# Head norms of a gated DeltaNet branch: sums over channels as two products with ones, and their way from tokens to a row

## The chip, the cores and the metric

One Trainium2 chip, one core. The time is that of one execution in device microseconds, as the median of repeated runs. The kernel takes the whole layer in one launch.

## The reference, cut to what matters

A hybrid encoder layer with three parallel branches (gated DeltaNet, latent attention, cross-attention to a memory) of width 1024 with 8 heads of 128 channels in the branch that matters here, for two inputs of 256 tokens each. The kernel treats both inputs as one stretch of 512 tokens. The change is in the last step of the DeltaNet branch: its output o is normed per head and token over the 128 channels, and then gated.

```python
def _rmsnorm(x, gain):
    xf = x.astype(jnp.float32)
    y = xf * lax.rsqrt(jnp.mean(xf * xf, axis=-1, keepdims=True) + EPS)
    return (y * gain.astype(jnp.float32)).astype(x.dtype)
...
o_gdn = _rmsnorm(o_fwd + o_bwd, gdn_norm_gain).reshape(b, s, W_GDN).astype(x.dtype) * jax.nn.silu(z_gdn)
...
merged = (gates[:, :, 0] * (o_gdn @ w_br_gdn) + gates[:, :, 1] * (o_mla @ w_br_mla) + gates[:, :, 2] * (o_mem @ w_br_mem))
return x + merged @ w_out
```

## The kernel before, in words

Nearly all values lie with channels on the 128 partitions and the 512 tokens along the row. Big products are made in three passes of a reduced float type: each operand is split into a high and a low part (`split`, L216: a ScalarE copy at L219 rounds to the high part, a VectorE subtraction at L221 or L223 gives the rest; weights in the same way at L207 and L211), and high*high, high*low and low*high are summed in PSUM. Such a product is one generator, `gemm` (L243 issues the matmuls, tiles `gm_...`); 24 matmuls of 128x512 make one output block of 128 channels.

The program has a front, a middle and a back (`run`). In the middle, `weave` merges seven chains (preparation, loads, the inner part of each head, two lanes that solve the recurrences, `heads_out`, `heads_norm`) with the stream of big products. Every chain yields two numbers: the TensorE time that it has just issued and how long to stay away. As long as no chain is due, `weave` issues the next matmul of the big products and moves its clock on by 0.234. TensorE's order is what `weave` writes down. The other engines' orders come from a scheduler that goes by priorities, which each chain sets as an offset (`heads_out` 2000, `heads_norm` 1500), and by `issue_after`, which keeps an instruction behind the last split of a weight (`wround`: its ScalarE half, `wsplit`: its VectorE half). Each engine then works strictly in its own order.

For each head hh, `gdn_out` (from L1100) does this:

- o, eight matmuls at L1117 in one PSUM bank; og = o * gain * z at L1124 (VectorE), o squared into sq at L1126 (ScalarE), a second square added at L1127 and L1129, so that the term with EPS is right; then the chain stays away for 11 (13 for head 7).
- so, the sums over channels, at L1133: for each block of 128 tokens a float32 matmul with sq as the stationary operand and a column of ones as the moving one. The trace counts eight weight loads and eight matmuls for the four. The result is 128x4, a token on each partition.
- rr at L1135 (VectorE, 128x4), to the power -0.5 at L1136 (GpSimd), turned in blocks of 32x32 at L285 (VectorE), so that four rows of each block of 32 partitions hold the tokens, and four DMAs from SyncE's queue at L287 put them in order into one row of the DRAM buffer `d_n`.

`gdn_norm` (from L1141) reads that row back to all 128 partitions (`rob`, a DMA that ScalarE issues at L292, behind `wround`), multiplies og by it at L1149 (behind `wsplit`), and splits the result into `xg` (L219, L223). `xg` is read in the back by the products `gm_bg`. The back starts when the last products `gm_bm` of the middle have been issued.

Small tiles share buffers by tags: `ta`, `tb` and `ct` have two buffers each of 128x512. `tb` holds sq and rob. `ct` holds the gates `gt_...` and `zt_...` on their way to DRAM, and `cz`, the raw tiles of the convolution (L733, L743). A new tile with a tag waits until everything that reads the tile before the last has ended.

Of the kernel before, what the change touches and what calls it, by code (L numbers as in the profile page):

```python
# [7 lines left out]
F32 = mybir.dt.float32  # L8
F32R = mybir.dt.float32r
AF = mybir.ActivationFunctionType  # L10
ALU = mybir.AluOpType
AX = mybir.AxisListType

P = 128
# [3 lines left out]
EPS = 1e-6  # L18
# [137 lines left out]
class Layer:  # L156
# [34 lines left out]
    def c(self, n):  # L191
        lo, hi = _OFF[n]
        return self.cst[:, lo:hi]
# [82 lines left out]
    def bcast(self, r, ps):  # L276

        for tb in range(4):
            self.nc.tensor.matmul(ps[:, tb * P:(tb + 1) * P], r[:, tb:tb + 1].to_broadcast([P, P]),
                                  self.c("id"), start=True, stop=True)  # L280

    def store_cols(self, r, i):

        nc = self.nc
        nc.vector.transpose(out=self.rt, in_=r)  # L285
        for b in range(4):
            nc.sync.dma_start(self.d_n[i].rearrange("(j b i) -> b j i", j=4, b=4)[b], self.rt[32 * b:32 * b + 4])  # L287

    def load_row(self, dst, i):

# [809 lines left out]
    def gdn_out(self, hh):  # L1100

        nc, pg, c = self.nc, self.pg, self.c
        par, kq = hh % 2, self.kq[hh]
        (na, es, vt), ub = self.hd[hh], self.ub[hh]

        op = self.ps_ms(par, f"o{hh}")
        o3 = op.rearrange("p (s t) -> p s t", s=2)
        for s in range(2):
            n = 0
            for d in range(2):  # L1110
                for cp in range(2):
                    if cp == 0:
                        out, rhs = o3[:, s], es[d][:, s, 0:256]
                    else:
                        lo = 128 * (1 - d)
                        out, rhs = o3[:, s, lo:lo + 128], es[d][:, s, 256:384]
                    nc.tensor.matmul(out, ub[:, d, s, cp], rhs, start=n == 0, stop=n == 3)  # L1117
                    n += 1
            yield 1.3, 0.0

        og = self.ta(f"og{hh}")
        nc.sync.dma_start(og, self.d_z[:, hh])
        self.out = hh + 1
        nc.vector.scalar_tensor_tensor(og, op, self.gg, og, ALU.mult, ALU.mult)  # L1124
        sq = self.tb(f"sq{hh}")
        nc.scalar.activation(sq, op, AF.Square)  # L1126
        nc.scalar.activation(kq[:, :, 1], kq[:, :, 1], AF.Square, scale=0.064)  # L1127
        s3 = sq.rearrange("p (s t) -> p s t", s=2)
        nc.vector.tensor_tensor(s3, s3, kq[:, :, 1], op=ALU.add)  # L1129
        yield 0.0, 13 if hh == 7 else 11  # L1130
        ssp = self.ps_ms(par, f"so{hh}")
        for tb in range(4):
            nc.tensor.matmul(ssp[:, tb:tb + 1], sq[:, tb * P:(tb + 1) * P], c("one"), start=True, stop=True)  # L1133
        rr = self.rr[:, 0:4]
        nc.vector.tensor_scalar(rr, ssp[:, 0:4], 1.0 / 128, 128 * EPS * EPS, ALU.mult, ALU.add)  # L1135
        nc.gpsimd.tensor_tensor(rr, rr, c("hf")[:, 0:4], op=ALU.pow)  # L1136
        self.store_cols(self.rr, hh)
        self.og[hh] = og, self.now + 10.0
        yield 0.9, 0.0

    def gdn_norm(self, hh):  # L1141

        nc = self.nc
        og = self.og[hh][0]
        rb = self.tb(f"rob{hh}")
        self.load_row(rb, hh)
        yield 0.0, 6.0
        with self.tc.issue_after(self.wsplit):
            nc.vector.tensor_tensor(og, og, rb, op=ALU.mult)  # L1149
        hl = self.pk.tile([P, 2, 512], F32R, tag="kq", bufs=8, name=f"xg{hh}")  # L1150
        self.split(og, hl[:, 0], hl[:, 1], 0.5)
        self.xg[hh] = hl[:, 0], hl[:, 1]
# [283 lines left out]
    def middle(self):  # L1436

        self.prepare(99)
        nc = self.nc
        fills = self.fills  # L1440

        self.ym = []
        for j in range(2):
            y = self.pg.tile([P, 2, 4, P], F32, tag=f"y{j}", bufs=1, name=f"y{j}")
            m = self.pg.tile([P, 2, P], F32, tag=f"m{j}", bufs=1, name=f"m{j}")
            nc.gpsimd.memset(y, 0.0)
            nc.gpsimd.memset(m, 0.0)
            self.ym.append((y, m))
        self.loads, self.loaded, self.started = {}, {}, set()
        self.og = {}  # L1450
        self.rr, self.rt = (self.p0.tile([P, 32], F32, name=n) for n in ("rr", "rt"))
        nc.gpsimd.memset(self.rr, 0.0)
        self.hd, self.ub, self.out, self.idle = {}, {}, 0, 0.0
        self.now, self.ready, self.pr = 0.0, {}, [None, None]
        with self.tc.manual_schedule(engines={mybir.EngineType.PE}):
            self.weave((self.preps(), 100), (self.heads_load(), 300), (self.heads_in(), 300), (self.lane(0), 2000), (self.lane(1), 2000),
                       (self.heads_out(), 2000), (self.heads_norm(), 1500))
# [153 lines left out]
```

## Time and profile before

| | before |
|---|---|
| median of 3 runs | 866.36 us (865.55 to 867.13) |
| profiled execution | 867.27 us, span 865.5 us, granted TensorE clock 0.995 |
| TensorE busy (PE) | 851.6 us of the span |
| VectorE busy (DVE) | 574.6 us |
| ScalarE busy (ACT) | 455.9 us |
| GpSimd busy (POOL) | 143.2 us |
| SyncE | issues DMAs only |

How to read it: PE is TensorE's matmul, PEld its weight loads, which overlap matmuls, DVE VectorE, ACT ScalarE, POOL GpSimd, SP SyncE; a letter q behind an engine's name is its queue of DMA issues. A row of the timeline gives the start, the duration of the whole group, the engine, the line, the operation with its output and inputs, its shape and how many instructions there are, and in brackets the idle time before it with what ended it. Matmuls are pipelined: a start is when a matmul begins, and the next one starts well before its end, so distances between starts tell what a matmul costs TensorE. A row of a group gives the line, engine, operation, shapes and count, then busy time in us, the mean of one in ns, and the idle time just before with its releaser.

### The profile page before, as it was taken

How to read it: one execution, taken by the hardware profiler on the slowest of the kernel's cores; microseconds unless marked ns; L12 is line 12 of the kernel's file. 1: busy time of each engine (PE TensorE's matmuls, PEld its weight loads, DVE VectorE, ACT ScalarE, POOL GpSimd, SP SyncE). 2: the span in 40 equal slices, each digit the busy share in tenths (PEclk: the TensorE clock that was granted, in tenths of full speed). 3: DMA queues.
4: the chain of work that ended last, by engine and by line, in shares of the span. 5: the costliest groups of instructions: out<-in, count | busy, mean ns of one | idle time of the engine just before them, and what ended most of it. 6: DMA issues, size and time to landing. Idle time of an engine off the chain costs nothing.

```text
span 865.5 us, 13255 instructions
## 1 busy us (share of the span) xinstructions
PE 851.6 (98%) x4854; PEld 703.0 (81%) x4854; DVE 574.6 (66%) x1013; ACT 455.9 (53%) x899; POOL 143.2 (17%) x135
## 2 busy tenths in 40 slices
PE   8999998999999999999999999999999999999997
PEld 6878887888888888878788888888888888888886
DVE  7776348876889865567689996765456543356543
ACT  7654454555655465545775647766563633223232
POOL 0200111000100100163011262303120002332121
PEclk9999999999999999999999999999999999999998
DMA  9322221452225423554232445544445436474432
GB/s 332 130 90 75 86 78 42 137 148 94 82 81 152 146 77 112 172 161 155 99 111 92 146 144 168 183 135 146 144 139 167 148 118 229 139 239 154 121 98 97
DMA packets 50864, 116.09 MB, mean 134 GB/s; under 512 B 7152, under 2 KB 12656, under 8 KB 50800
## 3 DMA queue, kind: packets, MB, share of 16 engines
q1 hardware_dynamic: 44896, 104.51, 38.1%
q10 hardware_dynamic: 5904, 10.75, 3.6%
q8 instruction: 38, 0.62, 0.3%
q14 instruction: 26, 0.21, 0.1%
HBM read 95.09 MB, written 16.99 MB: 130 GB/s over the span
## 4 chain that ended last, share of the span: by engine, by line
PE 94%; DVE 2%; DMA 2%; ACT 1%; issue 1%; POOL 0%; POOLq 0%; DVEq 0%; ACTq 0%; SPq 0%
PE gm_g L243 16%; PE gm_qkv L243 14%; PE gm_z L243 8%; PE gm_bm L243 5%; PE gm_bg L243 5%; PE gm_za L243 5%; PE y L1252 5%; PE gm_be L243 3%; PE gm_qm L243 3%; PE gm_km L243 3%; PE kk L967 3%; PE o L1117 2%; PE s_a L305 2%; PE vm L396 2%; PE gm_cq L243 2%; PE gm_qn L243 2%
## 5 line engine op out<-in xcount | busy, mean ns | idle before, releaser
L742 DVE SCALAR_TENSOR_TENSOR kq<-cz,prm,kq 128x510 f32<-128x510 f32 (+1 forms) x64 | 49.5, 773 | 11.6 <-ACT kq L735 10.9
L243 PE MATMUL gm_g<-hh,wl_g 128*128 128x512 f32 x192 | 51.8, 400 | 0.0
L243 PE MATMUL gm_g<-hh,wh_g 128*128 128x512 f32 x192 | 51.3, 401 | 0.5 <-ACT cz L733 0.5
L243 PE MATMUL gm_qkv<-hh,wl_qkv 128*128 128x512 f32 x192 | 51.6, 399 | 0.0
L243 PE MATMUL gm_qkv<-hh,wh_qkv 128*128 128x512 f32 x192 | 51.4, 406 | 0.0
L243 PE MATMUL gm_g<-hl,wh_g 128*128 128x512 f32 x192 | 50.4, 398 | 0.0
L211 DVE TENSOR_TENSOR wl_qkv<-wr_qkv,wh_qkv 128x1024 fp32r<-128x1024 f32 x24 | 31.4, 1308 | 27.7 <-PE gm_qkv L243 10.5
L243 PE MATMUL gm_qkv<-hl,wh_qkv 128*128 128x512 f32 x192 | 49.7, 396 | 0.0
L211 DVE TENSOR_TENSOR wl_g<-wr_g,wh_g 128x1024 fp32r<-128x1024 f32 x24 | 29.8, 1240 | 27.5 <-ACT wh_g L207 12.0
L243 PEld LDWEIGHTS gm_qkv<-hl,wh_qkv 128*128 128x128 f32 x192 | 35.8, 188 | 8.3
L243 PEld LDWEIGHTS gm_qkv<-hh,wh_qkv 128*128 128x128 f32 x192 | 36.0, 193 | 7.7
L243 PEld LDWEIGHTS gm_g<-hl,wh_g 128*128 128x128 f32 x192 | 35.5, 188 | 7.9
L243 PEld LDWEIGHTS gm_g<-hh,wh_g 128*128 128x128 f32 x192 | 35.1, 188 | 8.4 <-ACT cz L733 0.9
L243 PEld LDWEIGHTS gm_g<-hh,wl_g 128*128 128x128 f32 x192 | 35.2, 188 | 7.4
L243 PEld LDWEIGHTS gm_qkv<-hh,wl_qkv 128*128 128x128 f32 x192 | 35.2, 188 | 7.4
L1252 PE MATMUL y<-wh_wo,mh 128*128 128x512 f32 (+1 forms) x144 | 40.0, 370 | 0.0
L207 ACT ACTIVATE wh_qkv<-wr_qkv 128x1024 fp32r<-128x1024 f32 x24 | 25.3, 1056 | 24.6 <-PE gm_qkv L243 9.0
L1222 POOL TENSOR_TENSOR mg<-mg,lg 128x512 f32<-128x512 f32 x16 | 27.9, 1747 | 62.0 <-DVE lg L1221 62.0
L207 ACT ACTIVATE wh_g<-wr_g 128x1024 fp32r<-128x1024 f32 x24 | 25.3, 1055 | 17.7 <-PE gm_g L243 8.4
L957 POOL TENSOR_TENSOR kl<-kq,kh 128x512 fp32r<-128x512 f32 x16 | 23.0, 1441 | 64.3 <-ACT kh L955 64.2
L243 PE MATMUL gm_bm<-xa,wh_bm 128*128 128x512 f32 x128 | 32.9, 396 | 0.0
L243 PE MATMUL gm_bg<-xg,wh_bg 128*128 128x512 f32 x128 | 32.4, 395 | 0.0
(434 smaller groups left out, 2207.3 us busy)
## 6 DMA issues: line engine op xcount, KB each, us to landing
wr_qkv<-in_w_dram SPq DMA_DIRECT2D x24, 512.0 KB
wr_g<-in_w_dram SPq DMA_DIRECT2D x24, 512.0 KB
e<-d_r SPq DMA_DIRECT2D x64, 96.0 KB
wr_z<-in_w_dram SPq DMA_DIRECT2D x12, 512.0 KB
wr_za<-in_w_dram SPq DMA_DIRECT2D x8, 512.0 KB
d_g<-gt_g ACTq DMA_DIRECT2D x16, 256.0 KB
wr_bm<-in_w_dram SPq DMA_DIRECT2D x8, 512.0 KB
lg<-d_g SPq DMA_DIRECT2D x16, 256.0 KB
```

Of the source, the lines that this page charges most:

```text
L207: self.wround = nc.scalar.activation(hi[:, :n], raw[:, :n], AF.Copy).ins
L211: d = eng.tensor_tensor(lo[:, :n], raw[:, :n], hi[:, :n].bitcast(F32), op=ALU.subtract)
L243: nc.tensor.matmul(ps[:m], a[:, k * m:(k + 1) * m], xs[k][j], start=n == 0, stop=n == 3 * nk - 1)
L305: nc.tensor.matmul(sp[:, qb * 256:(qb + 1) * 256], a, b, start=j == 0, stop=j == n - 1)
L396: nc.tensor.matmul(vps[tb], ms[k][a][:, t], b[:, :512], start=k == 0 and i == 0, stop=k == 7 and i == 2)
L742: nc.vector.scalar_tensor_tensor(ys, zs, self.cw[:, f, m:m + 1], ys, ALU.mult, ALU.add)
L957: nc.gpsimd.tensor_tensor(lo, src, hi.bitcast(F32), op=ALU.subtract)
L967: nc.tensor.matmul(ps, a[:, k], b, start=i == 0, stop=i == 2)
L1117: nc.tensor.matmul(out, ub[:, d, s, cp], rhs, start=n == 0, stop=n == 3)
L1222: nc.gpsimd.tensor_tensor(self.merged[d], self.merged[d], gt, op=ALU.add)
L1252: nc.tensor.matmul(ps, xs[2 * j + q][a][:, t], b[:, q * 512 + c0:q * 512 + c1], start=j == 0 and n == 0, stop=j == 3 and n == 5)
```

## The change

The sum over channels turns round. sq is split into a high part `sh` and a low part `sl`; a matrix of ones, 128x32, made once at the start by ScalarE, is the stationary operand, and the two parts are the moving ones. The result is 32 equal rows of 512 tokens. The scaling (now 32x512) is done on VectorE. The tile is turned in blocks of 32x32 so that every block of 32 tokens stands on 32 partitions; GpSimd takes the power of one column of each of the 16 blocks (32x16, a stride of 32); after a stay of 6.0 the tile is turned back, behind `wsplit`, and one DMA writes row 0, now in the order of the tokens, to `d_n`. `store_cols`, `rr` and `rt` go. `sh` and the turned tile take buffers of the tag `ct`, `sl` and the scaled tile buffers of `tb`. The chain reports 0.47 of TensorE time instead of 0.9. `gdn_norm` keeps its code.

```diff
-    def store_cols(self, r, i):
-
-        nc = self.nc
-        nc.vector.transpose(out=self.rt, in_=r)
-        for b in range(4):
-            nc.sync.dma_start(self.d_n[i].rearrange("(j b i) -> b j i", j=4, b=4)[b], self.rt[32 * b:32 * b + 4])
...
         nc.vector.tensor_tensor(s3, s3, kq[:, :, 1], op=ALU.add)
+        hi = self.pk.tile([P, 512], F32R, tag="ct", bufs=2, name=f"sh{hh}")
+        lo = self.pk.tile([P, 512], F32R, tag="tb", bufs=2, name=f"sl{hh}")
+        self.split(sq, hi, lo)
         yield 0.0, 13 if hh == 7 else 11
-        ssp = self.ps_ms(par, f"so{hh}")
-        for tb in range(4):
-            nc.tensor.matmul(ssp[:, tb:tb + 1], sq[:, tb * P:(tb + 1) * P], c("one"), start=True, stop=True)
-        rr = self.rr[:, 0:4]
-        nc.vector.tensor_scalar(rr, ssp[:, 0:4], 1.0 / 128, 128 * EPS * EPS, ALU.mult, ALU.add)
-        nc.gpsimd.tensor_tensor(rr, rr, c("hf")[:, 0:4], op=ALU.pow)
-        self.store_cols(self.rr, hh)
+
+        ssp = self.ps_ms(par, f"so{hh}")[0:32]
+        nc.tensor.matmul(ssp, self.ones, hi, start=True, stop=False)
+        nc.tensor.matmul(ssp, self.ones, lo, start=False, stop=True)
+        ss, st = (self.pk.tile([P, 512], F32, tag=t, bufs=2, name=f"{t}s{hh}")[0:32] for t in ("tb", "ct"))
+        nc.vector.tensor_scalar(ss, ssp, 1.0 / 128, 128 * EPS * EPS, ALU.mult, ALU.add)
+        nc.vector.transpose(out=st, in_=ss)
+        nc.gpsimd.tensor_tensor(st[:, 0:512:32], st[:, 0:512:32], c("hf")[0:32, 0:1].to_broadcast([32, 16]), op=ALU.pow)
+        yield 0.47, 6.0
+        with self.tc.issue_after(self.wsplit):
+            nc.vector.transpose(out=ss, in_=st)
+        nc.sync.dma_start(self.d_n[hh:hh + 1], ss[0:1])
         self.og[hh] = og, self.now + 10.0
-        yield 0.9, 0.0
-
+        yield 0.0, 0.0
...
-        self.rr, self.rt = (self.p0.tile([P, 32], F32, name=n) for n in ("rr", "rt"))
-        nc.gpsimd.memset(self.rr, 0.0)
+        self.ones = self.p0.tile([P, 32], F32R, name="ones")
+        nc.scalar.activation(self.ones, self.c("one").to_broadcast([P, 32]), AF.Copy)
```

Line numbers behind `store_cols` fall by 7 in the changed kernel (L1088 becomes L1081, L292 becomes L285). In the changed kernel the matmuls stand at L1129 and L1130, the scaling at L1132, the two turns at L1133 and L1137, the power at L1134 and the DMA at L1138.

The order of the instructions, first on TensorE at the sums of head 2 (gm_qkv is a big product, hh and hl the parts of its right operand, wh its weight). Before:

```order
L243 MATMUL gm_qkv_5754<-hl_350,wh_qkv_5750 128x512
L243 MATMUL gm_qkv_5754<-hl_357,wh_qkv_5750 128x512
L1133 MATMUL so_5796<-cst,sq_5654 128x1 x4
L243 MATMUL gm_qkv_5754<-hl_364,wh_qkv_5750 128x512
L243 MATMUL gm_qkv_5754<-hl_371,wh_qkv_5750 128x512
```

And now:

```order
L243 MATMUL gm_qkv_5790<-hh_377,wh_qkv_5786 128x512
L243 MATMUL gm_qkv_5790<-hh_384,wh_qkv_5786 128x512
L1129 MATMUL so_5799<-sh_5644,ones 32x512
L1130 MATMUL so_5799<-sl_5645,ones 32x512
L243 MATMUL gm_qkv_5790<-hl_338,wh_qkv_5786 128x512
L243 MATMUL gm_qkv_5790<-hl_343,wh_qkv_5786 128x512
```

Two products take the place of four, four big matmuls earlier; before and after them stand big matmuls, as before. Behind the sums of heads 1 and 4 stands, before and now, a group of matmuls with 32x32 tiles (`p`, L1018); behind those of the other heads stand matmuls of 128x128 tiles, big ones or a lane's.

Second, VectorE at the norm of head 3 (w is read by the next matmuls us of a lane, xe, zt and wl are splits, a gate and a weight, og the multiplication by the row that came back). Before:

```order
L1135 TENSOR_SCALAR rr<-so_6269 128x4
L285 STREAM_TRANSPOSE rt<-rr 128x32
L1088 TENSOR_TENSOR w_6310<-vs_5299,xs_6307 128x256
...
L1159 SCALAR_TENSOR_TENSOR zt_z_6322<-zt_z_6322,gm_z_6256 128x512
L1149 TENSOR_TENSOR og_6146<-og_6146,rob_6388 128x512
L1088 TENSOR_TENSOR w_6373<-vs_5679,xs_6368 128x256
```

And now:

```order
L1132 TENSOR_SCALAR tbs_6281<-so_6278 32x512
L1133 STREAM_TRANSPOSE cts_6282<-tbs_6281 32x512
L1081 TENSOR_TENSOR w_6316<-vs_5300,xs_6313 128x256
L223 SCALAR_TENSOR_TENSOR xe_6331<-xe_6331 128x512
L211 TENSOR_TENSOR wl_z_6404<-wr_z_6400,wh_z_6402 128x1024
L223 SCALAR_TENSOR_TENSOR xe_6333<-xe_6333 128x512
L223 SCALAR_TENSOR_TENSOR xe_6335<-xe_6335 128x512
L1137 STREAM_TRANSPOSE tbs_6281<-cts_6282 32x512
...
L1081 TENSOR_TENSOR w_6381<-vs_5679,xs_6376 128x256
L211 TENSOR_TENSOR wl_g_6498<-wr_g_6494,wh_g_6496 128x1024
L1149 TENSOR_TENSOR og_6151<-og_6151,rob_6444 128x512
```

The turn that needs the power moves from second place to eighth behind the scaling, with five instructions of other work between the two turns, and og moves behind the second w.

Third, VectorE at the same place of head 4 in the changed kernel:

```order
L1132 TENSOR_SCALAR tbs_6589<-so_6586 32x512
L1133 STREAM_TRANSPOSE cts_6590<-tbs_6589 32x512
L1202 SCALAR_TENSOR_TENSOR gt_g_6554<-gt_g_6554,gm_be_6562 128x512
L211 TENSOR_TENSOR wl_be_6724<-wr_be_6720,wh_be_6722 128x512
L1137 STREAM_TRANSPOSE tbs_6589<-cts_6590 32x512
L223 SCALAR_TENSOR_TENSOR xa_6492<-xa_6492 128x512
L1081 TENSOR_TENSOR w_6671<-vs_5679,xs_6668 128x256
```

Here two instructions stand between the turns, and w stands behind the second turn.

Last, ScalarE's queue at the read of the row of head 7, the last one (wh_bm and wh_bg are high parts of weights, gm_bg's first among them, xg the high part of the normed output). Before:

```order
L207 ACTIVATE wh_bm_7597<-wr_bm_7595 128x1024
L207 ACTIVATE wh_bm_7633<-wr_bm_7631 128x1024
L292 DMA rob_7644<-d_n 128x512
L207 ACTIVATE wh_bg_7683<-wr_bg_7681 128x1024
L219 ACTIVATE xg_7667<-og_7479 128x512
```

And now:

```order
L207 ACTIVATE wh_bm_7610<-wr_bm_7608 128x1024
L207 ACTIVATE wh_bm_7648<-wr_bm_7646 128x1024
L207 ACTIVATE wh_bg_7698<-wr_bg_7696 128x1024
L285 DMA rob_7679<-d_n 128x512
L219 ACTIVATE xg_7682<-og_7490 128x512
```

The read of the row moves behind the first weight of `gm_bg`.

## The prediction, on record before the run

> **What bounds the kernel now.** I read the page's busy times first, then its chain of work that ended last, then the busy times in the stretch in which the changed code runs. First the page's line of busy times, and the line of the chain:
>
> ```profile
> PE 851.6 (98%) x4854; PEld 703.0 (81%) x4854; DVE 574.6 (66%) x1013; ACT 455.9 (53%) x899; POOL 143.2 (17%) x135
> PE 94%; DVE 2%; DMA 2%; ACT 1%; issue 1%; POOL 0%; POOLq 0%; DVEq 0%; ACTq 0%; SPq 0%
> ```
>
> The next row is the middle of the program, from 433 to 770 us. Its columns are PE, weight loads, DVE, ACT and POOL, each with its count, then the granted clock, DMA share and GB/s:
>
> ```profile
> 433.00:770.00 337.00, 337.00 (x2075) 279.44 (x2075) 220.63 (x408) 183.89 (x396) 73.31 (x65) 1.00 0.47 148
> ```
>
> TensorE sets the time. In the middle it works all 337.00 us at a granted clock of 1.00, while VectorE stands idle for 116 us, ScalarE for 153 and GpSimd for 264. So the change is worth what it takes out of TensorE's own order, less any time for which TensorE comes to wait. Work added elsewhere is free until a matmul needs its result.
>
> **What TensorE gives up.** The timeline of TensorE at the sums of head 2, and a stretch of plain big matmuls with which to compare it:
>
> ```profile
> 561.33 1.10 PE L243 MATMUL gm_qkv<-hl,wh_qkv 128*128 128x512 f32 x4
> 562.26 0.95 PE L1133 MATMUL so<-cst,sq 128*128 128x1 f32 x8
> 563.07 1.18 PE L243 MATMUL gm_qkv<-hl,wh_qkv 128*128 128x512 f32 x4
> 564.10 0.39 PE L243 MATMUL gm_qkv<-hh,wl_qkv 128*128 128x512 f32 x1
> ```
>
> ```profile
> 443.28 2.02 PE L243 MATMUL gm_qkv<-hl,wh_qkv 128*128 128x512 f32 x8
> 445.14 0.60 PE L1093 MATMUL us<-w,y 128*128 128x128 f32 x4
> ```
>
> Eight big matmuls take 445.14 − 443.28 = 1.86 us from start to start, 0.2325 each. From 561.33 to 564.10 are 2.77 us with eight big matmuls in them, so the sums of one head take 2.77 − 1.86 = 0.91 us. Behind the sums of heads 1 and 4 comes a group of 32x32 tiles:
>
> ```profile
> 527.00 0.95 PE L1133 MATMUL so<-cst,sq 128*128 128x1 f32 x8
> 527.87 0.45 PE L1018 MATMUL p<-t,na 32*32 32x32 f32 x32
> ```
>
> There 0.87 us go by from so to p, and 0.10 of them belong to the entry into the smaller tiles (worked out next), so 0.77. I take 0.91 for the six other heads, which rests on head 2. Together: 6 x 0.91 + 2 x 0.77 = 7.0 us.
>
> **What TensorE takes on.** Two matmuls per head with 512 moving columns in the reduced type, sixteen in all: 16 x 0.2325 = 3.7 us, if they flow like the big ones. They use 32 columns of the array. The trace has one other group of that tile, kd, in the same engine's timeline:
>
> ```profile
> 427.95 0.40 PE L806 MATMUL dp<-dr11ct,bd 128*128 128x512 f32 x1
> 428.28 1.30 PE L820 MATMUL kd<-kq 128*32 128x32 f32 x128
> 429.51 0.96 PE L243 MATMUL gm_g<-hl,wh_g 128*128 128x512 f32 x3
> 430.31 0.39 PE L243 MATMUL gm_g<-hh,wl_g 128*128 128x512 f32 x1
> ```
>
> Ahead of kd the last 128x128 matmul takes 0.33 us instead of 0.23: the entry costs 0.10. Behind it three big matmuls take 430.31 − 429.51 = 0.80 us instead of 0.70: the way back costs another 0.10. With eight entries and six exits (heads 1 and 4 go on to the small tiles of p, whose entry is paid in any case) this is 14 x 0.10 = 1.4 us. So the new sums cost 3.7 + 1.4 = 5.1 us, and TensorE saves 7.0 − 5.1 = 1.9 us. Without any cost of the change of tiles it would be 7.0 − 3.7 = 3.3; with double the price, 0.5. I take 1.9, because kd has the very shape of tile.
>
> The Trainium skill speaks against the change here: its page "TensorEngine Tiling (Array Packing)", section "Tiling Modes", says that a switch of the tiling mode drains TensorE. It gives no figure; kd's 0.33 against 0.23 agrees with it, and by it 1.9 stands rather than 3.3.
>
> **What the other engines take on.** The nearest rows, by groups on VectorE, then GpSimd, ScalarE and, from the timeline of the last head, SyncE:
>
> ```profile
> L221 DVE TENSOR_TENSOR pl_a<-pt_a,ph_a 128x512 fp32r<-128x512 f32 x16 | 10.9, 684 | 6.6 <-ACT ph_a L219 6.4
> L285 DVE STREAM_TRANSPOSE rt<-rr 128x32 f32<-128x32 f32 x8 | 1.7, 210 | 11.5 <-POOL rr L1136 11.5
> L857 DVE STREAM_TRANSPOSE ndt<-nd 128x512 f32<-128x512 f32 x2 | 1.4, 708 | 0.0
> L489 DVE TENSOR_TENSOR kru<-gm_kr,sin 32x512 f32<-32x512 f32 x2 | 1.4, 682 | 0.1
> L1135 DVE TENSOR_SCALAR rr<-so 128x4 f32<-128x4 f32 x8 | 1.3, 160 | 9.7 <-PE so L1133 9.6
> L389 DVE TENSOR_SCALAR wh_vm<-wr_vm 128x512 fp32r<-128x512 f32 x1 | 0.4, 427 | 2.2 <-DMA wr_vm<-in_wvm_dram 2.2
> ```
>
> ```profile
> L1136 POOL TENSOR_TENSOR rr<-rr,cst 128x4 f32<-128x4 f32 x8 | 8.1, 1011 | 99.1 <-DVE rr L1135 99.1
> L840 POOL TENSOR_TENSOR nk<-k,cst 128x16 f32<-128x16 f32 x2 | 5.8, 2896 | 92.1 <-DVE k L832 92.1
> ```
>
> ```profile
> L219 ACT ACTIVATE xg<-og 128x512 fp32r<-128x512 f32 x8 | 5.0, 630 | 12.5 <-DVE og L1149 12.4
> ```
>
> ```profile
> 757.30 1.28 SPq L287 DMA_DIRECT2D d_n<-rt  x4
> ```
>
> A scaling of 512 columns took 0.43 us out of SBUF; a 32x512 operation out of PSUM took 0.68. I take 0.68, since the new scaling reads PSUM, with 0.43 as the other end. Per head VectorE gets the low part 0.68, the scaling 0.68 and two turns at 0.71, and loses 0.16 and 0.21: +2.4 us, 19 over eight heads, against 116 idle. By the Trainium skill ("VectorE: DVE Perf Modes", section "Why PSUM operands drop a tier") a float32 operand in PSUM has no faster mode, which is how the two rows differ; at 0.43 the sum on VectorE would be 17.
>
> GpSimd's power on 16 columns cost 2.9 us on 128 partitions, on 4 columns 1.0. It now gets 16 columns on 32 partitions with a stride: between 1.0 and 2.9, and I take 2.9, because its two rows grow with columns. That is +1.9 per head, 15 in all against 264 idle. ScalarE gets one rounding, 0.63 per head, 5 in all against 153 idle. SyncE issues one DMA for four: 1.28 − 0.32 = 0.96 us less per head. The matrix of ones is one small ScalarE copy at the start for one memset; I count it at nothing, since its first readers, the sums of head 0, lie in the middle, beyond 433 us.
>
> **The way from the sums to og** becomes longer: scaling +0.5, two large turns for a small one 2 x 0.71 − 0.21 = +1.2, power +1.9, DMA issues −0.96: +2.6 us, and more where the second turn stands behind other work. Nothing in the middle reads the normed output; only gm_bg does. What can hurt is order: VectorE works strictly in turn, and its rows near the sums also make w for the lanes' matmuls. First og's row by groups, then VectorE at heads 3 and 4, then TensorE's us that reads each w:
>
> ```profile
> L1149 DVE TENSOR_TENSOR og<-og,rob 128x512 f32<-128x512 f32 x8 | 6.0, 753 | 9.9 <-DMA rob<-d_n 9.9
> ```
>
> ```profile
> 614.99 0.21 DVE L285 STREAM_TRANSPOSE rt<-rr 128x32 f32<-128x32 f32 x1 [4.79 <-POOL rr L1136]
> ...
> 623.34 0.41 DVE L1088 TENSOR_TENSOR w<-vs,xs 128x256 f32<-128x256 f32 x1
> ...
> 648.83 0.41 DVE L1088 TENSOR_TENSOR w<-vs,xs 128x256 f32<-128x256 f32 x1
> ```
>
> ```profile
> 623.80 0.71 PE L1093 MATMUL us<-w,y 128*128 128x128 f32 x4
> ...
> 652.82 0.61 PE L1093 MATMUL us<-w,y 128*128 128x128 f32 x4
> ```
>
> At head 3 w ended at 623.75, and us began 0.05 later: no room. At head 4 there were 3.6 us. Before, VectorE stood 11.5 us for the power and 9.9 us for the row that came back. Now other work lies between the turns (five instructions at head 3), which hides 2.9 us there, and the tight w at head 3 has moved ahead of og. Against this stand 2.4 us more of VectorE work per head, the thin cover at head 4, and the tag `ct`: its two buffers now also hold sh until the sums and the turned tile until the second turn, so a gate or cz on ScalarE may wait for these, and the first turn for a store to DRAM. I put this at 0.6 us of waiting on TensorE in all, an estimate: 0.3 at each of two places; nothing to 3.0 are the ends. A gain here is excluded, since TensorE had no idle time in the middle.
>
> **The end of the middle.** The row of head 7 goes on ScalarE's queue behind the first weight of gm_bg. ScalarE, then VectorE, then TensorE there:
>
> ```profile
> 759.47 0.33 ACTq L292 DMA_DIRECT2D rob<-d_n  x1
> 763.12 1.06 ACT L207 ACTIVATE wh_bg<-wr_bg 128x1024 fp32r<-128x1024 f32 x1 [4.54 <-PE gm_bm L243]
> ```
>
> ```profile
> 763.70 0.69 DVE L1149 TENSOR_TENSOR og<-og,rob 128x512 f32<-128x512 f32 x1 [3.65 <-DMA rob<-d_n]
> ...
> 766.04 1.78 DVE L223 SCALAR_TENSOR_TENSOR xg<-og,xg 128x512 fp32r<-128x512 f32 x1
> ```
>
> ```profile
> 774.12 0.62 PE L243 MATMUL gm_bg<-xg,wh_bg 128*128 128x512 f32 x2
> ```
>
> The weight ends at 764.18, so the read starts 4.7 us later than at 759.47, og comes at about 768.4 and the low part of xg ends at 767.82 + 4.7 = 772.5. The parts of head 7 are first needed at 774.12: covered by 1.6 us. Beyond that each us costs one.
>
> **Sum.** −1.9 on TensorE, +0.6 of waits: −1.3 us. The profiled execution took 867.27 us, 0.91 above the median of the runs shown; it would come to 866.0, and the median to 866.36 − 1.3 = 865.1 us. About 0.2% (1.7 us) is what a measurement of this kernel can tell from no change, so this is "the same". Its own range, with changes of tiles from 0.05 to 0.15 each and waits from 0 to 2, is 863.8 to 867.2.
>
> **Rivals.**
>
> A, the two products flow without a break. kd's 0.10 could come from its 128 tiny matmuls, and not from the tile. Then TensorE saves 3.3, less 0.6: 866.36 − 2.7 = 863.7 us, faster. For it: the weights of 32 columns are small. Against it: kd's entry costs 0.10 ahead of its first matmul, and as much again behind its last.
>
> B, slower, by VectorE's order. At heads where little lies between the turns, VectorE stands for the power, 2.9 us, and the w behind it comes late by that less its room, which went from 0.05 to 3.6 us; at 1.8, the middle, each such place costs 1.1 us. With four of eight heads so, 4.4 − 1.9 = +2.5: 868.9 us. It decides (slower by over 1.7) from (1.9 + 1.7) / 1.1 = 3.3 places on. For it: head 4's order, and that `ct` and `tb` make further waits. Against it: before, VectorE stood for 11.5 us at the same power with w behind it, and TensorE lost nothing.
>
> C, the end: og of head 7 more than 1.6 us later than worked out, as when the power or the second turn waits for a multiplication of 2 us on its engine. Then 3 us late cost 1.4, and the time is 866.5 us.
>
> D, the change does not shorten TensorE at all: the sums of the new kind cost 0.9 per head in all, as the old ones do (a switch of 0.2 each way). 866.36 + 0.6 = 867.0 us.
>
> **Chances.** Forecast 0.50, A 0.22, B 0.15, C 0.06, D 0.07. Faster by over 0.2% (below 864.6): A and a sixth of the forecast, 0.30. Slower (above 868.1): B and a third of C and D, 0.19. Within: 0.51. The range leaves out a third of A below (863.2) and two thirds of B above (868.4), 0.17 in all.
>
> **What would show it.** Right: so's group from start to the next matmul's start near 0.5 us, with gaps of 0.33 at the entry; TensorE still without idle time in the middle; DVE's busy time up by some 19 us and POOL's by 15. A is right if the start-to-start stays at 0.23. B shows as idle time of TensorE's us or kk with VectorE as releaser, C as idle time of gm_bg with xg as releaser. Wrong altogether would be a time that moves while TensorE's idle time and its sums do not.

## The result, and the profile after

The changed kernel took 873.17 us in the median of 4 runs (871.12 to 874.88); the kernel before took 866.75 us in 4 runs beside it (865.55 to 867.13). The ratio is 1.0075 with a 95% interval of 1.0063 to 1.0087: slower by 6.4 us, where 1.3 us faster was forecast. The profiled execution took 874.66 us, with a span of 872.8 us. Two of the four executions took 874.7 and 874.9 us at a granted clock of 0.994, the others 871.1 and 871.7 us at 0.996 and 0.995, so the size of the loss is known to some 2 us only.

The page of the changed kernel, the lines of busy time and of the chain that ended last:

```profile
PE 851.2 (98%) x4806; PEld 697.7 (80%) x4806; DVE 590.0 (68%) x1029; ACT 460.3 (53%) x908; POOL 158.9 (18%) x134
PE 79%; DVE 10%; DMA 4%; ACT 3%; issue 2%; POOL 1%; SPq 0%; POOLq 0%; DVEq 0%; ACTq 0%
```

The busy time of TensorE reads as before (851.6 then), but the chain no longer runs through TensorE alone: 15 of a hundred parts have gone to VectorE, DMA, ScalarE, GpSimd and to issue (time in which an engine waited for nothing that the profile shows). The middle shows why, in the same columns as before:

```profile
433.00:770.00 337.00, 329.01 (x1988) 268.04 (x1987) 231.12 (x416) 184.31 (x400) 85.28 (x63) 0.99 0.45 141
```

TensorE now stands for 8.0 us of the 337, and its clock was 0.99. In the next rows kk are products of keys in the inner part of a head, from which VectorE makes na and e (L971); p, u and xs are steps of a lane, of which ScalarE makes copies (p1s, u), and zt_z is a gate. By the code, the waits for zt_z, e and p1s are for a buffer in PSUM that the matmul is to write and that the named instruction still reads. The timeline of TensorE has these stalls in brackets:

```profile
525.84 0.74 PE L243 MATMUL gm_qkv<-hh,wh_qkv 128*128 128x512 f32 x2 [1.25 <-DVE zt_z L1159]
...
550.49 0.71 PE L1077 MATMUL xs<-u,m 128*128 128x128 f32 x4 [0.67 <-ACT u L1069]
...
555.08 0.47 PE L960 MATMUL kk<-kh 128*128 128x512 f32 x1 [3.18 <-DVE e L971]
...
556.39 3.25 PE L243 MATMUL gm_z<-hh,wh_z 128*128 128x512 f32 x8
...
568.77 0.42 PE L1129 MATMUL so<-sh,ones 128*32 128x512 f32 x1 [2.12 <-ACT p1s L1015]
```

Nearly all of it lies between 524 and 572 us, around the norm of head 1; one more, 0.7 us, comes at 657 us. The row at 556.39 shows a cost that no bracket names: eight big matmuls last 3.25 us there, where eight took 2.02 before. Some matmuls after the stalls run at half speed, 0.427 us from start to start.

The sums themselves became cheaper, and more so than forecast. TensorE at head 5:

```profile
682.52 0.85 PE L243 MATMUL gm_be<-xe,wh_be 128*128 128x512 f32 x3
683.21 0.40 PE L1129 MATMUL so<-sh,ones 128*32 128x512 f32 x1
683.44 0.39 PE L1130 MATMUL so<-sl,ones 128*32 128x512 f32 x1
683.68 1.33 PE L243 MATMUL gm_be<-xe,wh_be 128*128 128x512 f32 x5
```

Three big matmuls take 683.21 − 682.52 = 0.69 us, the two of the sums 683.68 − 683.21 = 0.47. The change of tiles costs nothing on the way in or out. So the new sums take 16 x 0.2325 = 3.7 us, against 7.0 before: 3.3 us are saved.

How that sums up, from the first kd matmul of the second group (428.28 before) to the first matmul of gm_bg, before and then after:

```profile
769.22 2.02 PE L243 MATMUL gm_bg<-xg,wh_bg 128*128 128x512 f32 x8
```

```profile
426.58 1.30 PE L813 MATMUL kd<-kq 128*32 128x32 f32 x128
...
776.57 3.43 PE L243 MATMUL gm_bg<-xg,wh_bg 128*128 128x512 f32 x14
```

Before it was 340.9 us, after 350.0: 9.1 longer. Over all matmul starts of the trace in this stretch, the seven gaps above 0.45 us exceed the usual pitch by 9.6 us together, and eleven matmuls at half speed by 2.2: 11.8 us. Less the 3.3 saved this is 8.5, which leaves 0.6 for small gaps. The whole execution grew by 7.4 us only, since the part ahead of this stretch took 1.7 us less. It took 1.3 to 1.7 us less in the profiles of e4, e12 and e13 too, which keep the old sums, so this is no gain of the change.

Where the stalls come from is read on VectorE's timeline, on the way of head 1 from its sums to og and on to e, which the matmuls kk of the next head wait for:

```profile
528.79 0.67 DVE L1132 TENSOR_SCALAR tbs<-so 32x512 f32<-32x512 f32 x1
535.28 0.70 DVE L1133 STREAM_TRANSPOSE cts<-tbs 32x512 f32<-32x512 f32 x1 [5.81 <-DMA d_xm<-zt_z]
...
541.55 0.70 DVE L1137 STREAM_TRANSPOSE tbs<-cts 32x512 f32<-32x512 f32 x1 [2.02 <-POOL cts L1134]
...
548.81 0.69 DVE L1149 TENSOR_TENSOR og<-og,rob 128x512 f32<-128x512 f32 x1 [3.50 <-DMA rob<-d_n]
...
550.08 0.73 DVE L971 SCALAR_TENSOR_TENSOR na<-e,cc,kk 128x256 f32<-128x256 f32 x2
550.73 1.20 DVE L735 SCALAR_TENSOR_TENSOR vf<-cz,prm,vf 128x508 f32<-128x508 f32 x1
551.85 1.78 DVE L223 SCALAR_TENSOR_TENSOR xg<-og,xg 128x512 fp32r<-128x512 f32 x1
553.55 0.47 DVE L971 SCALAR_TENSOR_TENSOR e<-e,cc,kk 128x256 f32<-128x256 f32 x1
```

VectorE stands three times on one way: 5.8 us until a gate has been stored (the turned tile takes its buffer in `ct`), 2.0 us for the power, 3.5 us for the row. All the work queued behind moves along. Between na and e stand a step of the convolution (vf) and the low part of the late og itself. They took 1.20 and 1.78 us, against 0.73 and 0.69 for most of their kind, which is 1.6 us of the delay of e; GpSimd worked on 128x512 tiles beside them (vs at 550.34, kl at 551.82), but that this slowed them was not tested.

ScalarE stands as well: first at cz, which waits for the turned tile's buffer, and later at the rounding of the late og, with u behind it, for which TensorE's xs waits 0.7 us. GpSimd's power took nearly twice its usual time here:

```profile
542.28 0.60 ACT L726 ACTIVATE cz<-gm_qkv 128x512 f32<-128x512 f32 x1 [3.69 <-DVE tbs L1137]
...
549.53 0.63 ACT L219 ACTIVATE xg<-og 128x512 fp32r<-128x512 f32 x1 [3.72 <-DVE og L1149]
550.07 0.36 ACT L1069 ACTIVATE u<-u 128x256 f32<-128x256 f32 x1
```

```profile
536.06 5.46 POOL L1134 TENSOR_TENSOR cts<-cts,cst 32x16 f32<-32x16 f32 x1 [8.27 <-DVE cts L1133]
```

At its end the middle went as worked out: the low part of the last xg ended at 779.33 and was needed from 781.47 on.

```profile
778.64 0.69 DVE L223 SCALAR_TENSOR_TENSOR xg<-og,xg 128x512 fp32r<-128x512 f32 x1 [0.70 <-ACT xg L219]
```

```profile
781.47 0.63 PE L243 MATMUL gm_bg<-xg,wh_bg 128*128 128x512 f32 x2
```

### The profile page after: what moved, and what is told of

Read it like the earlier page. It is cut to its first block, busy times and chain, and to the rows that moved or that the text cites. A ratio compares the mean times of both kernels' runs of the same rounds, so it can differ in the third digit from the quotient of the medians.

```text
span 872.8 us, 13163 instructions
## 1 busy us (share of the span) xinstructions
PE 851.2 (98%) x4806; PEld 697.7 (80%) x4806; DVE 590.0 (68%) x1029; ACT 460.3 (53%) x908; POOL 158.9 (18%) x134
## 4 chain that ended last, share of the span: by engine, by line
PE 79%; DVE 10%; DMA 4%; ACT 3%; issue 2%; POOL 1%; SPq 0%; POOLq 0%; DVEq 0%; ACTq 0%
PE gm_g L243 13%; PE gm_qkv L243 11%; PE gm_bg L243 5%; PE gm_bm L243 5%; PE gm_za L243 5%; PE y L1252 4%; PE gm_z L243 4%; PE vm L389 3%; PE gm_qm L243 3%; PE gm_km L243 3%; PE gm_be L243 2%; PE s_a L298 2%; PE gm_cq L243 2%; DMA e<-d_r 2%; PE kk L960 2%
## 5 line engine op out<-in xcount | busy, mean ns | idle before, releaser
L1134 POOL TENSOR_TENSOR cts<-cts,cst 32x16 f32<-32x16 f32 x8 | 27.0, 3375 | 107.0 <-DMA mg<-d_m 46.3
```

The costliest lines, as they stand in the source:

```text
L1134: nc.gpsimd.tensor_tensor(st[:, 0:512:32], st[:, 0:512:32], c("hf")[0:32, 0:1].to_broadcast([32, 16]), op=ALU.pow)
```

## The experiments

Theory 1 at first was: the buffers of `ct`, which the new tiles share with gates and cz, make VectorE and ScalarE wait, and the stalls follow. Theory 2: the longer way and the added work do it by themselves. Times are compared as ratios to the kernel before on the same chip.

| run | what | time, us | ratio to before (95% interval) |
|---|---|---|---|
| changed | as above | 873.17 | 1.0075 (1.0063 to 1.0087) |
| e1 | no new tile in ct or tb | 867.86 | 1.0015 (1.0006 to 1.0024) |
| e2 | turned tile out of ct | 866.97 | 1.0004 (0.9994 to 1.0015) |
| e3 | sh out of ct | 869.61 | 1.0041 (1.0027 to 1.0055) |
| e4 | before, with the split added | 866.87 | 1.0003 (0.9994 to 1.0012) |
| e5 | e1 without turns and power | 864.21 | 0.9976 (0.9967 to 0.9984) |
| e6 | e1 with a power of 4 columns | 866.06 | 0.9996 (0.9987 to 1.0005) |
| e7 | e2 with sums later | 864.53 | 0.9982 (0.9969 to 0.9994) |
| e8 | e2 with quarter turns | 864.89 | 0.9984 (0.9975 to 0.9993) |
| e9 | e8 with sums later | 864.84 | 0.9982 (0.9973 to 0.9991) |
| e10 | e9 with sh and sl exchanged | 867.38 | 1.0010 (1.0001 to 1.0019) |
| e11 | changed, sums later | 866.90 | 1.0003 (0.9994 to 1.0012) |
| e12 | before, its turned tile in ct | 866.65 | 1.0004 (0.9995 to 1.0013) |
| e13 | before, sums later | 867.50 | 1.0009 (1.0000 to 1.0018) |
| e14 | changed, sums later still | 874.83 | 1.0088 (1.0067 to 1.0108) |
| e15 | changed, row and og later | 868.00 | 1.0019 (1.0006 to 1.0033) |
| e16 | changed, og not waiting for its row | 868.89 | 1.0029 (1.0019 to 1.0040) |

### The buffers: e1, e2, e3

These runs move the new tiles to places where something has just been used up. e1 puts sh and sl into the tile that later takes xg, and turns in place in sq:

```diff
-        hi = self.pk.tile([P, 512], F32R, tag="ct", bufs=2, name=f"sh{hh}")
-        lo = self.pk.tile([P, 512], F32R, tag="tb", bufs=2, name=f"sl{hh}")
+        hl = self.pk.tile([P, 2, 512], F32R, tag="kq", bufs=8, name=f"xg{hh}")
+        hi = hl[:, 0]
+        lo = hl[:, 1]
...
-        ss, st = (self.pk.tile([P, 512], F32, tag=t, bufs=2, name=f"{t}s{hh}")[0:32] for t in ("tb", "ct"))
+        ss = st = sq[0:32]
```

> The changed kernel, but none of the new tiles takes a buffer of ct or tb: sh and sl lie in the tile that later takes xg, the scaled rows lie in sq itself and are turned in place. Theory 1 (the shared buffers of ct make VectorE and ScalarE wait, and the rest follows from that): the first turn of head 1 no longer waits 5.8 us for a store, the sums keep their saving of about 3 us on TensorE, and the time is 863.5 to 865.5 us, faster than before by 1 to 3. Theory 2 (the longer way, 2.9 us of power, two turns, and 2.4 us of VectorE work per head are enough by themselves): it stays at 870 to 873 us.

e2 moves the turned tile alone, and e3 sh alone, as e1 does:

```diff
-        ss, st = (self.pk.tile([P, 512], F32, tag=t, bufs=2, name=f"{t}s{hh}")[0:32] for t in ("tb", "ct"))
+        ss = self.pk.tile([P, 512], F32, tag="tb", bufs=2, name=f"tbs{hh}")[0:32]
+        st = kq[0:32, 1].rearrange("p a t -> p (a t)")
```

> The changed kernel, but only the turned tile leaves the tag ct (it lies in the spent k and q of the same head); sh stays in ct, sl and the scaled rows in tb. Theory 1, in the form that the turned tile is what hurts: no wait of the first turn for a store, no wait of cz for the second turn; 864.5 to 867 us. If sh in ct, or tb, hurts as much: 868 to 871. Theory 2: 870 to 873.

> The changed kernel, but only sh leaves the tag ct; the turned tile stays in it. Theory 1, in the form that the turned tile is what hurts: head 1's first turn still waits about 6 us, 870 to 873 us. If sh is what shifts the buffers: 865 to 868. Theory 2: 870 to 873.

Measured: 867.86, 866.97 and 869.61 us. The turned tile out of `ct` takes back all of the loss, sh out of it about half; theory 2 in its plain form falls, and so does theory 1's number for e1: with no shared buffer at all it was still 1.3 us slower than before. In e3 the turned tile stays in `ct`, and still the first wait at head 1 is gone (the turn at 532.80 has none); TensorE's wait of 2.0 us at kk stands one head earlier there, behind a wait of 2.8 us at the second turn of head 0, as in e1. So e3 does not tell what a wait for `ct` at head 1 costs. VectorE's waits in e2 show that the first wait is gone and the others are not (in the rows of waits stand the total in us, how many there are, and the longest):

```profile
DVE og L1150 <- DMA rob<-d_n: 15.4, 6, 4.4
...
DVE tbs L1138 <- POOL kq L1135: 3.0, 1, 3.0
```

In e1 VectorE stood 2.8 us at the second turn of head 0, because GpSimd's order had put 3.6 us of other work ahead of the power, and it stood 2.1 us at og for the row; TensorE's kk waited 2.0 us behind these.

### Parts alone on the kernel before: e4, e12, e13

e4 adds only the split, its result unused:

```diff
         nc.vector.tensor_tensor(s3, s3, kq[:, :, 1], op=ALU.add)
+        hl = self.pk.tile([P, 2, 512], F32R, tag="kq", bufs=8, name=f"xg{hh}")
+        self.split(sq, hl[:, 0], hl[:, 1])
```

> The kernel before, with the split of sq into two parts added and its result unused (it lies in the tile that later takes xg); sums and way back as before. This is the price of the added 0.63 us on ScalarE and 0.68 us on VectorE per head alone. Theory 1: they fit in idle time, 866 to 867.5 us. Theory 2: part of the loss shows here, 868 to 870.

e12 gives the old way back a buffer of `ct` for its turned tile:

```diff
-        nc.vector.transpose(out=self.rt, in_=r)
+        rt = self.ct(f"rt{i}")[:, 0:32]
+        nc.vector.transpose(out=rt, in_=r)
```

> The kernel before with one thing changed: the turned 128x32 tile of the old way back takes a buffer of ct in place of its own. Sums, power and DMAs as before. Theory 1 (a turned tile in ct makes VectorE wait for stores to DRAM, whatever the sums): VectorE waits several us at the turn of one or two heads, and the time is 868 to 872 us. If the loss needs the longer way of the changed kernel: 866 to 867.5.

e13 keeps the old kernel and moves its sums:

```diff
-        yield 0.0, 13 if hh == 7 else 11
+        yield 0.0, 13 if hh == 7 else 12
```

> The kernel before with the stay ahead of the sums raised from 11 to 12 (as in e11), nothing else. If e11's gain over the changed kernel is of the changed kernel's own waits: 866 to 867.2 us, as before. If any shift of the sums by four big matmuls is good for some us by itself: 862 to 865.

All three stay within 0.1% of before. The added rounding and subtraction are hidden. A later place of the sums is worth nothing in the old kernel. And a turned tile in `ct` does no harm where the stores are in time: at head 1 of e12 the turn waited only for the power, and at head 6, where it waited 2.8 us for a store, TensorE lost nothing.

```profile
529.23 0.21 DVE L286 STREAM_TRANSPOSE rt<-rr 128x32 f32<-128x32 f32 x1 [1.12 <-POOL rr L1137]
```

SyncE's queue tells the difference. The store of the gate was issued at 525.49 before and at 530.41 in the changed kernel, where GpSimd's order has kl ahead of the gate's multiplication, which the store waits for, and SyncE's order two more loads ahead of the store, the first of them issued only at 528.90. First before, then changed:

```profile
525.49 0.42 SPq L1177 DMA_DIRECT2D d_xm<-zt_z  x1
```

```profile
530.41 0.42 SPq L1177 DMA_DIRECT2D d_xm<-zt_z  x1
```

So e12 refutes theory 1 as I had put it: the shared buffer by itself is not the loss.

### The way back: e5, e6, e8

e5 is e1 without the lines of the two turns and the power. e6 is e1 with this:

```diff
-        nc.gpsimd.tensor_tensor(st[:, 0:512:32], st[:, 0:512:32], c("hf")[0:32, 0:1].to_broadcast([32, 16]), op=ALU.pow)
+        nc.gpsimd.tensor_tensor(st[:, 0:128:32], st[:, 0:128:32], c("hf")[0:32, 0:1].to_broadcast([32, 4]), op=ALU.pow)
```

e8 computes everything with a short power (ss and st as in e2, the stationary ones as 128 columns):

```diff
+        for q in range(4):
+            nc.vector.transpose(out=st[32 * q:32 * q + 32, 0:128], in_=ss[32 * q:32 * q + 32, P * q:P * q + P])
+        nc.gpsimd.tensor_tensor(st[:, 0:128:32], st[:, 0:128:32], c("hf")[:, 0:4], op=ALU.pow)
...
+            nc.vector.transpose(out=st[:, 128:256], in_=st[:, 0:128])
+        nc.sync.dma_start(self.d_n[hh].rearrange("(q i) -> q i", q=4), st[0:128:32, 128:256])
```

> The kernel of e1_no_shared without the two turns and the power: row 0 of the scaled sums goes to DRAM as it is (so og is multiplied by the wrong factor; the power -0.5 is left out). It keeps the split, the two products and the shorter issue of one DMA. Theory 1 (TensorE's saving of about 3.3 us is real, and what is left of the loss in e1 and e2 comes from the wait for the power and from the later og): 863.3 to 864.8 us. Rival (the saving does not reach the time, by the price of the new products or by where they stand in TensorE's order): 866 to 868 us, with idle time of TensorE at so.

> The kernel of e1_no_shared with the power taken of 4 of the 16 columns (the other 12 are left as they are), so that it should last 1.0 us instead of 2.9. Theory 1 in the form that the length of the power is what is left: 864.5 to 866.5 us, and VectorE no longer stands 2.8 us at the second turn of head 0. If the two turns, the late og and the order of the queues do it without the power: 867 to 868.5.

> A version of e2_turn_moved with a short power: the sums come out equal on all 128 partitions, each group of 32 partitions turns only its own 128 tokens (four turns of 32x128), the power is taken of 128x4, one turn of 128x128 goes back, and one DMA writes four rows of 128. Sums, split and result as in the changed kernel. If the length of the power matters: 864.5 to 866.5 us. If not: 866.5 to 868.

Measured: 864.21, 866.06 and 864.89 us, each within what theory 1 had expected. e5 shows that the saving reaches the time: 0.24% or 2.1 us faster, of 3.3 saved, with one stall left on TensorE.

```profile
PE so L1130 <- ACT p1s L1015: 1.8, 1, 1.8
```

The length of the power counts: e6 is 1.9 thousandths below e1 by the ratios, about 1.6 us, e8 2.0 below e2 (its turns differ too). In e8 the power took 1.0 us as before the change:

```profile
L1136 POOL TENSOR_TENSOR kq<-kq,cst 128x4 f32<-128x4 f32 x8 | 8.2, 1025 | 105.4 <-DVE kq L1135 105.4
```

e8's sums are of 128x128 tiles, and TensorE gave them 0.23 to 0.24 us each, as it gave those of 128x32 in the changed kernel. What is left there of stalls is 1.2 us at zt_z and 0.7 at the sums of head 2.

### The place of the sums: e7, e9, e10, e11, e14

These change the stay ahead of the sums, and e10 the buffers of sh and sl. e7 is e2 with 12 in place of 11, e9 is e8 with it, e11 the changed kernel with it; e14 has 13 for every head. e10 is e9 with sh in `tb` and sl in `ct`.

```diff
-        yield 0.0, 13 if hh == 7 else 11
+        yield 0.0, 13 if hh == 7 else 12
```

> The kernel of e2_turn_moved with the stay ahead of the sums raised from 11 to 12, which puts them about four big matmuls later in TensorE's order. If the sums of head 2 wait 1.3 us for p1s because they were moved forward: that wait goes, 865 to 866.2 us. If the wait comes from late loads of e alone: it stays near 1.3 or moves to the next reader, 866.5 to 867.5.

> e8_quarter_turns and e7_sums_later together: short power, no turned tile in ct, sums four big matmuls later. If the two gains add up: 863.2 to 864.6 us, faster than before by 2 to 3. If each only shifted the same wait: 864.6 to 866.

> e9_quarter_later with the places of sh and sl exchanged (sh in tb, sl in ct). If TensorE's wait of 1.2 to 1.4 us for the gate zt_z near 525 us comes from sh standing ahead of it in ct: that wait goes, and the time is 0.5 to 1.3 us below e9's. If the new VectorE work ahead of zt_z does it: as e9, within 0.5.

> The changed kernel with the stay ahead of the sums raised from 11 to 12 and nothing else; the turned tile stays in ct. If the waits for the buffers of ct carry the loss: 869 to 873 us. If the place of the sums in TensorE's order carried it: 865 to 867.

> The changed kernel with the stay ahead of the sums at 13 for every head. If later sums help since they give og of head 1 cover from the wait for its row: as e11 or better, 864.5 to 867.5 us. If e11 was a lucky order of the queues: anywhere from 867 to 873.

Measured: e7 864.53, better than expected. The wait of head 2's sums for p1s is gone in it and in e9. That stall, 2.1 us in the changed kernel, has two causes by the trace, of which e7 and e9 test the first alone: the new order has the sums four big matmuls, 0.9 us, earlier, and SyncE's queue has the load of a weight ahead of the last two of eight loads of e, through which ScalarE's queue reaches p1s later. e9 did not add up: 864.84, the same as e8, since the stall at zt_z grew from 1.2 to 1.4 us and a new one of 0.4 came at a lane's u. e10 was a miss: the stall at zt_z fell to 0.5 us (from start to start), but others appeared and it came to 867.38. TensorE waited for zt_z in eight of the nine profiles with sh in `ct` and the new sums (not in e15), and in none with sh elsewhere save that 0.5 of e10.

e11 was the largest miss. The change of one number takes the loss of the changed kernel away (866.90 us), though VectorE still stands 5.2 us at the first turn:

```profile
DVE cts L1133 <- DMA d_xm<-zt_z: 5.2, 1, 5.2
```

And e14, one step further, is at 874.83 us, although that wait is down to 2.0:

```profile
DVE cts L1133 <- DMA d_xm<-zt_z: 2.0, 1, 2.0
```

So neither the first wait nor the place of the sums carries the loss by itself. What e14 and the changed kernel have in common is a stall of TensorE at kk of over 2 us, with a wait of VectorE at og of head 1 or 2 for its row just ahead of it; at these heads e11 waits 0.8 us at most. In e14 it is head 2; in VectorE's timeline there are 3.7 us of wait, then the next head's work up to e:

```profile
586.18 0.69 DVE L1149 TENSOR_TENSOR og<-og,rob 128x512 f32<-128x512 f32 x1 [3.73 <-DMA rob<-d_n]
...
590.21 0.74 DVE L971 SCALAR_TENSOR_TENSOR na<-e,cc,kk 128x256 f32<-128x256 f32 x2
...
592.43 0.73 DVE L971 SCALAR_TENSOR_TENSOR e<-e,cc,kk 128x256 f32<-128x256 f32 x2
```

TensorE waits for just that (and, 5 us earlier, 1.9 us at xs for ScalarE's u, which stands behind the rounding of the same late og):

```profile
PE kk L960 <- DVE e L971: 2.7, 1, 2.7
```

In e11 og of head 1 came at 547.91 without a wait, because more of cz's work stood ahead of it, and kk waited 0.9 us in two pieces. A wait at og is not enough by itself. At head 3 e11 has one of 5.0 us, with na 1.3 us behind og, and TensorE does not wait there; at head 1 e2 has one of 4.4 us, with og 5 us earlier than in the changed kernel (543.51), and TensorE loses 0.3 us to e. The wait costs where the e behind it is already due.

### The row: e15, e16

e15 makes read and og due later (14.0 for 10.0 after the sums). e16 leaves the changed kernel as it is, but og no longer depends on its row:

```diff
-            self.nc.scalar.dma_start(dst, self.d_n[i:i + 1].to_broadcast([P, 512]))
+            self.nc.scalar.dma_start(dst, self.d_z[0:1, i].to_broadcast([P, 512]))
```

> The changed kernel with the read of the row and og due 14.0 instead of 10.0 after the sums; sums where they were. If VectorE's wait of 3.5 us at og of head 1, ahead of the work that head 2's kk needs, makes the stall of 3.4 us on TensorE: that stall goes and the time is 866 to 869 us. If the wait for the store at the first turn does it alone: 870 to 873.

> The changed kernel, with one thing left out: og no longer waits for its own row, since rob is read from a row of the gates in DRAM that lies there long before (og is multiplied by the wrong factor). Split, products, turns, power and the DMA of the row stay as they are, and so do the buffers; VectorE's order differs only at heads 1 and 7, where og moves forward. If VectorE's wait for the row at og, ahead of the next head's work for kk, makes the stalls of 3.4 us on TensorE and, through the late release of og's buffer, the late loads of e: the time is 865 to 868.5 us though VectorE still waits some 5 us at the first turn. If the wait for the store at the first turn makes the loss by itself: 870 to 873 us.

Measured: 868.00 and 868.89 us. In e15 the wait at the first turn had gone as well (0.4 us), so it decides little. e16 is clearer: VectorE's order differs from the changed kernel's only at heads 1 and 7, where og and its split come earlier, and the first two waits stay at 5.5 and 2.8 us:

```profile
535.39 0.70 DVE L1133 STREAM_TRANSPOSE cts<-tbs 32x512 f32<-32x512 f32 x1 [5.51 <-DMA d_xm<-zt_z]
...
538.12 0.67 DVE L1149 TENSOR_TENSOR og<-og,rob 128x512 f32<-128x512 f32 x1
...
542.26 0.70 DVE L1137 STREAM_TRANSPOSE tbs<-cts 32x512 f32<-32x512 f32 x1 [2.81 <-POOL cts L1134]
```

The stall at kk has gone from TensorE, and the loss falls from 0.75% to 0.29%, by about 4 us. TensorE's waits in the middle are two:

```profile
PE so L1129 <- ACT p1s L1015: 2.6, 1, 2.6
...
PE gm_qkv L243 <- DVE zt_z L1159: 1.4, 1, 1.4
```

So the chain in the changed kernel is: the first wait does its harm mainly through the third. It makes the row of head 1 late; with e2 (first wait gone) or e16 (third gone) the stall at kk goes. The third can also come without the first: at head 2 of e14 the turns waited 0.2 us at most, but the row was read 4.4 us after the issue of the DMA that wrote it (582.05 after 577.62), against 1.2 us at head 1 of the changed kernel, and why stays open. The rest of the loss, with the saving counted against it, are the stalls at head 2's sums and at zt_z, which by the trace come from the new orders and are there in e16 too. I had also suspected the late release of og's buffer, which keeps a load on SyncE's queue in front of the loads of e. e16 speaks against it: og is early there, and the sums of head 2 wait as long.

## Why the prediction was wrong

The step that decided was the term of the waits: 0.6 us on TensorE were forecast, and 11.8 were measured. A smaller step, the price of a change of tiles, failed to the good side.

- **"0.6 us of waiting on TensorE in all, an estimate".** This term was mis-sized, and it turned the sign: the 11.8 us are 9.6 of stalls and 2.2 of matmuls at half speed, of which the sum had no term. The kinds of wait were named (the tag `ct`, "the first turn for a store", cz on ScalarE), but none was priced; VectorE's wait for the store alone took 5.8 us.
- **"Nothing in the middle reads the normed output; only gm_bg does."** True of data and wrong of the queue: VectorE stands at og until the row is there, and the next head's na and e stand behind it. Before, this wait was there too (9.9 us in five places) and cost TensorE nothing. I read from this that it had room, and did not ask what would be behind og when the row came some 9 us later: og of head 1 ran at 539.46 us before and at 548.81 after.
- **The way from sums to og, +2.6.** At head 1, from scaling to og, it became 20.0 us (528.79 to 548.81) from 9.6 (529.85 to 539.46): +10.4. The prices of the single steps held: scaling 0.68, turns 0.70, power 2.9 in six of eight heads.
- **What TensorE takes on.** Forecast 5.1 us with 0.10 for each change of tiles, measured 3.7. kd's gaps were taken as the price of its tile shape, and they are not. Rival A had this right. That its time, 863.7, comes out nearly in e5 (864.21) is in part luck: e5 leaves out the turns and the power, and has 1.8 us of waits where A has 0.6. What makes kd's and p's first gaps was not tried.
- **Rival B** named the right engine and kind (VectorE standing in its order, with the lanes' or the heads' work behind), and its sign, idle time of kk with VectorE as releaser, is there. But it put this at head 4, with 1.1 us a place. The price is not per place of a 2.9 us power; it came at one head, where three waits lie on one way.
- **Hidden work.** The split was hidden, as forecast (e4); the turns and the power were not (e5 against e1). VectorE's busy time rose by 15.4 us (19 forecast), GpSimd's by 15.7 (15). The end of the middle was covered: 1.6 us forecast, 2.1 measured.
- **Confidence.** The forecast held TensorE at no idle time because it had none before. In the changed kernel one constant at 11, 12 and 13 gives 873.2, 866.9 and 874.8 us. A range for a change that rewrites the order of five queues ought to have been set by that spread, which no row of before shows.

A version better than both is e7 or e8, the turned tile out of `ct` and the sums later or the power short: 0.18% and 0.16% faster than before, with intervals that exclude no change. The part of e5 that they do not reach, 0.06 to 0.08%, lies within these intervals.

## What to carry to other kernels

When TensorE is full and all else waits in order, price a change in a side chain by the longest stand that it can cause at an engine's head, and then read what is queued behind that instruction, rather than who reads its result. A tile that takes a turn in shared buffers inherits the DMA of whoever had the buffer before; look up when that transfer was issued. Before a saving of some tenths of a per cent is judged, try two or three neighbouring schedules: here one constant moved the time by 8 us.

## What the runs showed of the hardware

- A change from 128x128 to 128x32 tiles with 512 moving columns cost TensorE nothing: 0.23 us at entry and exit (rows of head 5 above). Ahead of the 32x32 tiles of p it was 0.32 us, behind 128x32 tiles in the changed kernel as behind 128x128 tiles in e8. The Trainium skill, page "TensorEngine Tiling (Array Packing)", section "Tiling Modes", says that a switch of mode drains the engine; no price of that is seen at these sums. The 0.32 ahead of p and the 0.33 ahead of kd stay unexplained.
- GpSimd's power took 2.9 us for 16 columns on 32 partitions, the same on 128 partitions before, and 1.0 us for 4 columns: here its time went by columns. Twice it lasted longer, 5.46 and 4.08 us, and why was not tried.
- After some stalls of TensorE, matmuls ran at 0.427 us, half speed, for up to ten matmuls: from start to start, after 2.4 us in e1, 2.5 in the changed kernel and 3.0 in e16. After 3.1 us in e15 and 2.1 in e1 none did. The granted clock in the changed kernel from 550 to 560 us was 0.83, the third number from the right in this row of busy times:

```profile
550.00:560.00 10.00, 6.28 (x21) 4.38 (x22) 9.95 (x18) 5.57 (x13) 3.46 (x4) 0.83 0.34 91
```

The Trainium skill, page "TensorE: Matmul & The Clock Gate", section "What's actually happening", has the clock halved after an idle window of about 3.4 us; here shorter stalls sufficed at times, which differs from it, and one of 3.1 us did not, which fits it.
